# Low parts of the state-space input weights: computed beside the first MLP and loaded from DRAM

## The chip, the cores and the metric

One core of a Trainium2 chip runs the whole program in one launch. The metric is the device time of one execution in microseconds, from the median of several runs. TensorE (PE) does the matmuls, VectorE (DVE), ScalarE (ACT) and GpSimd (POOL) the elementwise work, and SyncE's queue (SP) issues every DMA of the kernel before the change. Each engine takes its instructions in the order in which they are written into its queue; a waiting instruction holds up all that stand behind it.

## The reference, cut to what matters

A trunk of two layers on 512 tokens of width 1024, in float32. Layer 0 is attention and an MLP, layer 1 a state-space mixer and an MLP:

```python
for i in range(DEPTH):                      # DEPTH = 2
    mix = attention_mixer(x, ...) if i % 2 == 0 else mamba2_bidir_mixer(x, ...)
    x = layer_norm(DN_ALPHA * x + mix, ln1_g[i], ln1_b[i])
    x = layer_norm(DN_ALPHA * x + squared_relu_mlp(x, mlp_w1[i], mlp_w2[i]), ln2_g[i], ln2_b[i])

def squared_relu_mlp(x, w1, w2):            # 1024 -> 4096 -> 1024
    return jnp.square(jax.nn.relu(x @ w1)) @ w2

def mamba2_bidir_mixer(x, w_in, ...):
    zxbcdt = x @ w_in                       # 1024 -> 6208: the state-space input weights
    z, xbc, dt = jnp.split(zxbcdt, ...)
    xbc = jax.nn.silu(depthwise_conv_centred(xbc, conv_w, conv_b))
    ...                                     # one chunked scan per direction, gate, grouped norm
    return y @ w_out
```

## The kernel before

Every float32 matmul is made of three float32r matmuls: both operands are split into a high part (a rounded copy) and a low part (what the rounding left), and `split3` (L208) adds high times high, high times low and low times high into one PSUM bank. The weights are streamed as 219 chunks of 128x1024 float32 (512 KB), in the order of their use: chunks 0 to 25 for attention, 26 to 89 for the first MLP, 90 for the time steps (half a chunk), 91 to 138 for the state-space input projection, 139 to 154 for its output projection, 155 to 218 for the second MLP. One chunk feeds 24 matmuls of 512 columns.

`Weights.prepare` (L54) brings one chunk in: SP loads `w_raw`, ACT copies it to `w_hi` (L69), and DVE subtracts to get `w_lo` (L70); for the chunks listed in `ON_POOL` (L27) POOL does that subtraction. Chunks sit in a pool of four buffers; `more_weights` (L261) opens a second pool beside it, of four buffers in the first MLP, so that eight chunks are on their way there. In the state-space stage only the four are left.

`Main` (L250) holds the token-major phases. `sweep` (L274) multiplies and adds into the residual, `norm` (L328) is the layer norm of one tile of 128 tokens (its `rstd` on POOL, L336; the scaling on DVE, L340 and L343), `transpose` turns a normed tile for the next phase, with its low part taken on DVE at L232, `first_tiles` begins the next phase while the last tokens are still being normed, and `mlp` (L375) runs four quarters of eight up chunks and eight down chunks.

`ssd` (L757) is the state-space stage, eight groups. In each group the 48 projection chunks of the stage are fed to PE between the group's own small matmuls, in an order fixed by a table of step numbers (L971). POOL makes the decay differences `e` and `tb` from rows `r` that DMAs broadcast from `ac_d` (L865 to L875), the masks `m` and `tu` (L984 to L987) and the chunk states `pv` (L1064); DVE makes the convolutions (L801), `cbl` and `cbu` (L1025, L1026), the weighted inputs `xw` (L1046), and the sum into `pv` (L1067). A grouped norm goes through DRAM: `rs_d` is written and read back (L938, L939), and DVE L947 waits for it.

PE's order is the order of the code. The other engines' orders, and SP's, are set by a scheduler at build time; a change in any of their work moves what stands around it.

Of the kernel before, what the change touches and what calls it, by code (L numbers as in the profile page):

```python
# [40 lines left out]
class Weights:  # L41
    """Weight chunks of [128, 1024] float32, streamed in order and split exactly into two float32r parts."""

    def __init__(self, nc, pool, sources, ahead, in_order):
        self.in_order = in_order
        self.nc = nc
        self.pools = [pool]
        self.ahead = ahead
        self.sources = sources
        self.ready = []  # L50
        self.wide_until = 0
        self.at = 0

    def prepare(self, after=(), between=None):  # L54
# [7 lines left out]
        n = src.shape[1]  # L62
        raw = pool.tile([P, 1024], F32, name="w_raw")
# [14 lines left out]

    def widen(self, pool, extra, n):
        """Has a second pool of so many buffers take its share of the next n chunks to be used."""  # L80
# [13 lines left out]
class Slots:  # L94
    """Room for the two parts of eight [128, 512] operand tiles."""
# [16 lines left out]
def tile_encoder_trunk(ctx: ExitStack, tc: tile.TileContext, a: dict, out: bass.AP, stop=None):  # L112
# [14 lines left out]
    def banks_of(stack, counts):  # L127
        """Further PSUM banks: counts maps a name to its number of banks."""
# [11 lines left out]
    def in_order(ins, first):  # L140
        """Has an engine issue ins behind first."""
# [92 lines left out]
    def sweep_lead(yh, yl, banks, chunks, n, first=0):  # L234
        """Chunks of y @ W into four banks, K tile by K tile."""
# [13 lines left out]
    # ------------------------------------------------------------------ token-major phases  # L249
    class Main:  # L250
# [23 lines left out]
        def sweep(self, yh, yl, scale_res, finish=None, begun=None, within=None, between=None):  # L274
            """res <- [ALPHA *] res + y @ W for the K tiles in yh/yl; finish(t) when a token tile is done,
            within() late in the last one."""
# [83 lines left out]
        def first_tiles(self, n, m=P, then=None):  # L360
            """The next phase's first n projections, by token halves while the last tokens get done."""
# [39 lines left out]
        def overlapped(self, then=None):  # L401
            """Has token tiles 0 and 1 turned while 2 and 3 are computed."""
# [9 lines left out]
    # ------------------------------------------------------------------ layer 0: attention  # L412
    def attention(stack):
        """Returns the eight operand tiles of the output projection and its first sweep, begun."""
# [50 lines left out]
        # value rows of the neighbourhood heads, gathered into the column blocks' windows  # L465
# [17 lines left out]
        # keys and values of the windowed heads  # L483
# [240 lines left out]
    # ------------------------------------------------------------------ layer 1: SSD mixer  # L724
# [3 lines left out]
    def step_sizes(main, ps):  # L728
        """dt_tok <- softplus(dt + bias), tokens on partitions; wdec <- dt * -exp(A_log)."""
# [563 lines left out]
```

## Time and profile before

| | |
|---|---|
| runs, us | 1487.74, 1493.44, 1494.26 (median 1493.44) |
| span of the profiled execution, us | 1492.0 |
| PE busy | 1408.6 us, 94% of the span |
| DVE, ACT, POOL busy | 883.1, 583.6, 448.6 us |
| moved by DMA | 161.37 MB, 108 GB/s over the span |

The span runs from the first to the last instruction of one profiled execution; its own time outside the profiler is not given, so the span stands for it, 1.4 us under the median. Busy PE time counts pipelined matmuls and can't fall much; what can be lost or won lies in the 6% in which PE waits, and in the stage where it does. Waits are put down to the instruction that came last. Of the stages, attention ends at about 230 us, the first MLP at about 590, the state-space stage's groups run from about 640 to 1040, and the second MLP ends the program.

### The profile page before, as it was taken

The numbers are of one execution on the slowest core, as the hardware profiler recorded it, in microseconds if no ns is written. First come the engines' busy times: TensorE is split into PE (matmuls) and PEld (weight loads), VectorE is DVE, ScalarE is ACT, GpSimd is POOL, SyncE is SP. The second block draws the span as 40 slices with busy tenths as digits, with TensorE's granted clock in tenths as the row PEclk, the third lists the DMA queues.
The fourth block names the chain that finished last, engine by engine and source line by source line (L and its number), as shares of the span: only waits on it lengthen the run. The fifth ranks groups of instructions, "written<-read, shape, count | busy, mean of one in ns | idle before, by whom it ended". The sixth has DMA issues, their size and how long they took to land.

```text
span 1492.0 us, 18850 instructions
## 1 busy us (share of the span) xinstructions
PE 1408.6 (94%) x7200; PEld 1160.6 (78%) x7200; DVE 883.1 (59%) x1267; ACT 583.6 (39%) x899; POOL 448.6 (30%) x347
## 2 busy tenths in 40 slices
PE   8899999999999999978888997898998999999997
PEld 7777778888888888866777776776888888888886
DVE  4577576444343437598788788977467444243336
ACT  5688633223132321444444545452324323142220
POOL 1354230000000121276576777665333100000000
PEclk9999999999999999999999999998999999999999
DMA  8322255323232212363434443321436333143101
GB/s 286 104 87 63 71 200 168 99 90 95 68 129 86 78 56 78 117 195 100 138 110 125 130 134 121 99 89 43 139 109 226 99 99 99 57 128 99 57 1 57
DMA packets 62259, 161.37 MB, mean 108 GB/s; under 512 B 9596, under 2 KB 19480, under 8 KB 62168
## 3 DMA queue, kind: packets, MB, share of 16 engines
q1 hardware_dynamic: 62168, 160.16, 34.2%
q8 instruction: 57, 0.93, 0.3%
q14 instruction: 34, 0.28, 0.1%
HBM read 154.73 MB, written 5.39 MB: 107 GB/s over the span
## 4 chain that ended last, share of the span: by engine, by line
PE 70%; DVE 10%; POOL 7%; DMA 6%; issue 4%; SPq 2%; ACT 1%; DVEq 0%; POOLq 0%; ACTq 0%
PE mm L209 17%; PE mm L210 17%; PE mm L211 16%; PE b L211 4%; PE b L210 4%; PE b L209 4%; DMA r<-ac_d 4%; POOL m L987 1%; DVE w_lo L70 1%; DVE xw L1046 1%; POOL tu L985 1%; DVE res L343 1%; DVE lo L232 1%; POOL m L984 1%; SPq L509 1%
## 5 line engine op out<-in xcount | busy, mean ns | idle before, releaser
L69 ACT ACTIVATE w_hi<-w_raw 128x1024 fp32r<-128x1024 f32 (+1 forms) x220 | 231.6, 1054 | 585.6 <-PE mm L210 279.7
L209 PE MATMUL mm<-hi,w_hi 128*128 128x512 f32 (+2 forms) x1112 | 431.1, 388 | 0.6 <-ACT hi L231 0.5
L210 PE MATMUL mm<-lo,w_hi 128*128 128x512 f32 (+2 forms) x1112 | 421.2, 379 | 10.2 <-DVE lo L232 10.2
L211 PE MATMUL mm<-hi,w_lo 128*128 128x512 f32 (+2 forms) x1112 | 418.8, 377 | 0.0
L70 DVE TENSOR_TENSOR w_lo<-w_raw,w_hi 128x1024 fp32r<-128x1024 f32 (+1 forms) x182 | 235.1, 1294 | 266.4 <-ACT w_hi L69 265.8
L210 PEld LDWEIGHTS mm<-lo,w_hi 128*128 128x128 f32 (+1 forms) x1112 | 213.4, 192 | 44.2 <-DVE lo L232 10.9
L209 PEld LDWEIGHTS mm<-hi,w_hi 128*128 128x128 f32 (+1 forms) x1112 | 213.1, 192 | 41.1 <-issue 5.3
L211 PEld LDWEIGHTS mm<-hi,w_lo 128*128 128x128 f32 (+1 forms) x1112 | 212.9, 191 | 39.6
L70 POOL TENSOR_TENSOR w_lo<-w_raw,w_hi 128x1024 fp32r<-128x1024 f32 (+1 forms) x38 | 94.2, 2481 | 448.9 <-ACT w_hi L69 442.9
L209 PE MATMUL mm<-w_hi,hi 128*128 128x512 f32 x352 | 142.2, 404 | 5.7 <-ACT hi L171 5.0
L211 PE MATMUL mm<-w_hi,lo 128*128 128x512 f32 x352 | 140.3, 398 | 1.6 <-DVE lo L232 1.6
L210 PE MATMUL mm<-w_lo,hi 128*128 128x512 f32 x352 | 140.2, 398 | 0.0
L210 PE MATMUL b<-w_lo,hi 128*128 128x512 f32 (+1 forms) x328 | 123.5, 377 | 0.6 <-DVE w_lo L70 0.6
L211 PE MATMUL b<-w_hi,lo 128*128 128x512 f32 (+1 forms) x328 | 123.5, 376 | 0.0
L209 PE MATMUL b<-w_hi,hi 128*128 128x512 f32 (+1 forms) x328 | 123.5, 376 | 0.0
L336 POOL TENSOR_TENSOR rstd<-ve,half 128x1 f32<-128x1 f32 x16 | 12.5, 784 | 328.3 <-DVE neg L334 310.2
L209 PEld LDWEIGHTS mm<-w_hi,hi 128*128 128x128 f32 x352 | 67.4, 191 | 20.9 <-ACT hi L171 5.0
L211 PEld LDWEIGHTS mm<-w_hi,lo 128*128 128x128 f32 x352 | 67.3, 191 | 18.1 <-DVE lo L232 2.5
L210 PEld LDWEIGHTS mm<-w_lo,hi 128*128 128x128 f32 x352 | 67.4, 192 | 14.3
L384 DVE TENSOR_TENSOR sq<-relu 128x512 f32<-128x512 f32 x64 | 60.3, 943 | 28.7 <-ACT relu L382 28.7
L210 PEld LDWEIGHTS b<-w_lo,hi 128*128 128x128 f32 x328 | 61.8, 188 | 13.0 <-DVE w_lo L70 1.0
L209 PEld LDWEIGHTS b<-w_hi,hi 128*128 128x128 f32 x328 | 61.7, 188 | 12.0
(284 smaller groups left out, 1952.0 us busy)
## 6 DMA issues: line engine op xcount, KB each, us to landing
w_raw<-in_w_m_dram SPq DMA_DIRECT2D x128, 512.0 KB, 3.6
w_raw<-in_w_ssm_dram SPq DMA_DIRECT2D x48, 512.0 KB, 3.6
r<-ac_d SPq DMA_DIRECT2D x64, 256.0 KB, 4.5
w_raw<-in_w_so_dram SPq DMA_DIRECT2D x16, 512.0 KB, 3.5
w_raw<-in_w_att_dram SPq DMA_DIRECT2D x14, 512.0 KB, 4.9
r<-ac_d SPq DMA_DIRECT2D x64, 96.0 KB, 2.9
w_raw<-in_w_ao_dram SPq DMA_DIRECT2D x8, 512.0 KB, 3.7
xraw<-in_xT_dram SPq DMA_DIRECT2D x8, 256.0 KB, 6.4
```

Of the source, the lines that this page charges most:

```text
L69: split = [nc.scalar.activation(hi[:, cols], raw[:, cols], AF.Copy), eng.tensor_tensor(lo[:, cols], raw[:, cols], hi[:, cols].bitcast(F32) ...
L70: eng.tensor_tensor(lo[:, cols], raw[:, cols], hi[:, cols].bitcast(F32), op=ALU.subtract)]
L209: PE.matmul(ps, lhs_h, rhs_h, start=first, stop=False)
L210: PE.matmul(ps, lhs_h, rhs_l, start=False, stop=False)
L211: PE.matmul(ps, lhs_l, rhs_h, start=False, stop=last)
L232: return DVE.tensor_tensor(lo, src, hi.bitcast(F32), op=ALU.subtract)
L343: self.last = DVE.scalar_tensor_tensor(self.res[t][:, cols], u, rstd, self.b[:, cols], op0=ALU.mult, op1=ALU.add),
L384: DVE.tensor_tensor(s, r, r, op=ALU.mult)
L509: nc.sync.dma_start(out=vj[r * 32:r * 32 + 32, j, kt, :], in_=vb_g[kt * 4 + r, NA_START[j]:NA_START[j] + 32, pair * P:pair * P + P])
L984: POOL.tensor_tensor(m, cbl, bc(dt_tok[:, :, hf:hf + 1], full), op=ALU.mult)
L985: POOL.tensor_tensor(t, cbu, bc(dt_tok[:, :, 32 + hf:33 + hf], full), op=ALU.mult)
L987: POOL.tensor_tensor(m, m, es[h], op=ALU.mult)
```

## The change

The low parts of the 48 chunks 91 to 138 are no longer subtracted when they are used. While the first MLP runs, each call of `prepare` also takes one step of a generator, `split_beside`: SP loads a state-space chunk (`pre_raw`), ACT makes its high part (`pre_top`), POOL subtracts (`pre_low`), and SP stores the result in DRAM (`w_low`). Two buffers of each serve these steps; to make room, the second weight pool of the first MLP shrinks from four buffers to two. In the state-space stage SP loads `w_raw` and ACT makes `w_hi` as before, and a DMA issued by POOL loads `w_lo` from DRAM. `ON_POOL` is unchanged; its entries for chunks 91 to 138 have no more use. The docstrings and comments that the diff removes are left out here.

```diff
     def __init__(self, nc, pool, sources, ahead, in_order):
...
+        self.split_at = {}
+        self.beside = None
...
         n = src.shape[1]
+        if self.beside is not None:
+            next(self.beside, None)
+        if self.at - 1 in self.split_at:
+            raw = pool.tile([P, 1024], F32, name="w_raw")
+            hi = pool.tile([P, 1024], F32R, name="w_hi")
+            lo = pool.tile([P, 1024], F32R, name="w_lo")
+            nc.gpsimd.dma_start(out=lo, in_=self.split_at[self.at - 1])
+            nc.sync.dma_start(out=raw, in_=src)
+            nc.scalar.activation(hi, raw, AF.Copy)
+            self.ready.append((hi, lo))
+            return
...
+    def split_beside(self, pool, dram, indices):
+
+        nc = self.nc
+        for i in indices:
+            src = self.sources[i]
+            raw = pool.tile([P, 1024], F32, name="pre_raw")
+            top = pool.tile([P, 1024], F32R, name="pre_top")
+            low = pool.tile([P, 1024], F32, name="pre_low")
+            nc.sync.dma_start(out=raw, in_=src)
+            nc.scalar.activation(top, raw, AF.Copy)
+            nc.gpsimd.tensor_tensor(low, raw, top.bitcast(F32), op=ALU.subtract)
+            kept = dram.tile([P, 1024], F32, name=f"w_low{i}")
+            nc.sync.dma_start(out=kept, in_=low)
+            self.split_at[i] = kept
+            yield
...
-            main.more_weights(4, 68)
+            main.more_weights(2, 68)
...
             main.sweep(yh, yl, True, begun=begun, **main.overlapped())
+            pre = tc.tile_pool(name="pre", bufs=2)
+            weights.beside = weights.split_beside(pre.__enter__(), dram, range(91, 139))
...
+            run(weights.beside)
+            weights.beside = None
+            pre.__exit__(None, None, None)
```

What the scheduler makes of it stands at three places; the numbers of lines differ between the two programs. PE's order is the same in both, row for row.

POOL between attention and the first MLP, before. The four `rstd` are those of the four token tiles after attention, and the `w_lo` are chunks 26 to 29:

```order
L336 TENSOR_TENSOR rstd<-ve,half 128x1
L70 TENSOR_TENSOR w_lo<-w_raw,w_hi 128x1024 x2
L336 TENSOR_TENSOR rstd<-ve,half 128x1 x2
L70 TENSOR_TENSOR w_lo<-w_raw,w_hi 128x1024 x2
L336 TENSOR_TENSOR rstd<-ve,half 128x1
```

The same place of the same queue, now:

```order
L365 TENSOR_TENSOR rstd<-ve,half 128x1
L83 TENSOR_TENSOR w_lo<-w_raw,w_hi 128x1024 x2
L102 TENSOR_TENSOR pre_low<-pre_raw,pre_top 128x1024
L365 TENSOR_TENSOR rstd<-ve,half 128x1
L102 TENSOR_TENSOR pre_low<-pre_raw,pre_top 128x1024
L365 TENSOR_TENSOR rstd<-ve,half 128x1
L102 TENSOR_TENSOR pre_low<-pre_raw,pre_top 128x1024
L83 TENSOR_TENSOR w_lo<-w_raw,w_hi 128x1024 x2
L365 TENSOR_TENSOR rstd<-ve,half 128x1
```

Three of the new subtractions have come to stand between the norms; one is ahead of the second tile's `rstd`, and after the third tile's `rstd` three subtractions follow where there were two.

SP in the first MLP, before, is one run of loads:

```order
L271 DMA ln_g<-in_ln_dram 128x1024
L272 DMA ln_b<-in_ln_dram 128x1024
L68 DMA w_raw<-in_w_m_dram 128x1024 x52
L68 DMA w_raw<-in_w_dt_dram 128x512
```

Now stores and loads of the new steps stand between them (twelve rows out of its middle):

```order
L104 DMA w_low_3513<-pre_low 128x1024
L100 DMA pre_raw<-in_w_ssm_dram 128x1024
L81 DMA w_raw<-in_w_m_dram 128x1024
L104 DMA w_low_3558<-pre_low 128x1024
L100 DMA pre_raw<-in_w_ssm_dram 128x1024
L104 DMA w_low_3603<-pre_low 128x1024
L100 DMA pre_raw<-in_w_ssm_dram 128x1024
L104 DMA w_low_3648<-pre_low 128x1024
L100 DMA pre_raw<-in_w_ssm_dram 128x1024
L104 DMA w_low_3693<-pre_low 128x1024
L100 DMA pre_raw<-in_w_ssm_dram 128x1024
L104 DMA w_low_3738<-pre_low 128x1024
```

Each store waits for POOL's subtraction, and the next load of the pair stands behind it; from the first `pre_raw` to the last store there are 48 steps and 44 loads of MLP chunks, and the last 15 MLP chunks are loaded behind the last store.

POOL in one group of the state-space stage, now; the DMA rows are new, and the subtractions of `w_lo` that stood in this queue and in DVE's are gone:

```order
L1016 TENSOR_TENSOR m<-m,e 128x512
L901 TENSOR_TENSOR e<-r,ac_tok 128x512
L71 DMA w_lo<-w_low_4283 128x1024
L1093 TENSOR_TENSOR pv_7801<-pv_7771,cdec 128x512
L901 TENSOR_TENSOR e<-r,ac_tok 128x512
L903 TENSOR_TENSOR tb<-r,ac_tok 128x512 x2
L71 DMA w_lo<-w_low_4328 128x1024
L959 TENSOR_TENSOR rstd<-rstd,half 128x4
```

Such a DMA waits until PE has done with the chunk that held its buffer, four chunks earlier, and the group's own work on POOL stands behind it.

## Rows read from the trace of the kernel before

**Rows 1.** The page: busy time by engine, and the chain that ended last.

```profile
PE 1408.6 (94%) x7200; PEld 1160.6 (78%) x7200; DVE 883.1 (59%) x1267; ACT 583.6 (39%) x899; POOL 448.6 (30%) x347
PE 70%; DVE 10%; POOL 7%; DMA 6%; issue 4%; SPq 2%; ACT 1%; DVEq 0%; POOLq 0%; ACTq 0%
```

**Rows 2.** Windows: stretch, length, busy PE, PEld, DVE, ACT, POOL; clock, DMA share, GB/s.

```profile
180.00:235.00 55.00, 47.79 (x292) 39.99 (x292) 42.13 (x75) 18.14 (x31) 17.33 (x11) 0.94 0.51 172
235.00:545.00 310.00, 310.00 (x1427) 256.30 (x1426) 131.76 (x143) 97.33 (x124) 14.41 (x6) 1.00 0.29 93
545.00:640.00 95.00, 90.68 (x553) 79.38 (x551) 55.60 (x97) 25.32 (x34) 21.91 (x16) 1.00 0.34 105
640.00:985.00 345.00, 302.90 (x1653) 246.20 (x1654) 283.03 (x332) 168.84 (x232) 244.81 (x184) 0.96 0.42 124
```

**Rows 3.** PE's waits from 640 to 985 us: total us, times, longest.

```profile
PE aux L1056 <- DVE xw L1046: 16.0, 12, 2.3
PE aux L899 <- DVE cbu L1026: 11.6, 5, 3.9
PE aux L899 <- ACT xs L811: 6.1, 1, 6.1
PE aux L916 <- DVE pv L1067: 4.9, 3, 4.1
```

**Rows 4.** Groups of DVE and POOL, 640 to 985 us: count, busy us, mean ns, idle before.

```profile
L70 DVE TENSOR_TENSOR w_lo<-w_raw,w_hi 128x1024 fp32r<-128x1024 f32 x34 | 49.9, 1467 | 1.5 <-ACT w_hi L69 1.5
...
L987 POOL TENSOR_TENSOR m<-m,e 128x512 f32<-128x512 f32 x27 | 45.0, 1671 | 11.0 <-DVE m L986 11.0
L874 POOL TENSOR_TENSOR tb<-r,ac_tok 128x512 f32<-128x512 f32 x30 | 37.8, 1261 | 52.4 <-DMA r<-ac_d 46.8 <-DVE w_lo L70 3.1 <-DVE r L999 2.4
...
L70 POOL TENSOR_TENSOR w_lo<-w_raw,w_hi 128x1024 fp32r<-128x1024 f32 x5 | 12.9, 2573 | 2.6 <-ACT w_hi L69 2.6
...
L930 POOL TENSOR_TENSOR rstd<-rstd,half 128x4 f32<-128x4 f32 x6 | 6.1, 1021 | 2.4 <-DVE rstd L929 2.4
```

**Rows 5.** The chain that ended last, by line, 640 to 985 us.

```profile
by line: DMA r<-ac_d 13.9%; issue 10.9%; POOL m L987 5.8%; PE mm L209 5.3%; POOL tu L985 5.2%; PE mm L210 5.0%; PE mm L211 4.7%; POOL m L984 4.4%; DVE xw L1046 4.0%; POOL tb L874 3.8%; POOL pv L1064 3.3%; DVE w_lo L70 3.1%; POOL e L872 2.9%
```

**Rows 6.** DVE and PE around one group's start: start us, us, then idle before.

```profile
844.78 2.18 DVE L947 SCALAR_TENSOR_TENSOR hi<-hi,nw,q 128x512 f32<-128x512 f32 x2 [1.04 <-DMA q<-rs_d]
...
850.12 1.88 DVE L70 TENSOR_TENSOR w_lo<-w_raw,w_hi 128x1024 fp32r<-128x1024 f32 x1
...
857.49 2.09 DVE L1046 TENSOR_TENSOR xw<-xtok,wdec 128x384 f32<-128x384 f32 x2
859.63 1.38 PE L1056 MATMUL aux<-xw,btok 128*128 128x128 f32 x10 [0.83 <-DVE xw L1046]
```

**Rows 7.** Attention's last norms: DVE, then POOL, then PE.

```profile
214.67 1.41 DVE L343 SCALAR_TENSOR_TENSOR res<-ln_u,rstd,ln_b 128x512 f32<-128x512 f32 x2
...
220.49 5.28 DVE L343 SCALAR_TENSOR_TENSOR res<-ln_u,rstd,ln_b 128x512 f32<-128x512 f32 x2
219.95 5.26 POOL L70 TENSOR_TENSOR w_lo<-w_raw,w_hi 128x1024 fp32r<-128x1024 f32 x2
227.53 0.58 PE L210 MATMUL mm<-lo,w_hi 128*128 128x256 f32 x1 [5.29 <-DVE lo L232]
```

**Rows 8.** First MLP: two drains one chunk apart; ACT's copies; DMA landings; one SP issue.

```profile
304.35 0.69 DVE L310 SCALAR_TENSOR_TENSOR res<-res,b 128x512 f32<-128x512 f32 x1 [3.23 <-PE b L211]
309.89 0.69 DVE L310 SCALAR_TENSOR_TENSOR res<-res,b 128x512 f32<-128x512 f32 x1 [4.85 <-PE b L211]
L69 ACT ACTIVATE w_hi<-w_raw 128x1024 fp32r<-128x1024 f32 x56 | 59.4, 1061 | 207.2 <-PE mm L210 97.5 <-PE b L211 53.8 <-PE mm L211 50.9
w_raw<-in_w_m_dram SPq DMA_DIRECT2D x128, 512.0 KB, 3.6
res<-in_x_dram SPq DMA_DIRECT2D x4, 512.0 KB, 6.1
229.75 0.33 SPq L271 DMA_DIRECT2D ln_g<-in_ln_dram  x1
```

## The prediction on record

> **What bounds the kernel now.** I began with the page: PE is busy for 94% of the span and holds 70% of the chain that ended last [rows 1]. What PE does isn't touched, so the question is where it waits. The windows by stage answer that [rows 2]. In the first MLP PE never stops: 310 of 310 us, with the DMA engines at a 0.29 share, ACT busy for a third and POOL for a twentieth of the time. There is room for other work, but also nothing to win. In the state-space stage, 640 to 985 us, PE is busy for 302.9 of 345 us, so some 42 us are lost; DVE is busy for 283.0 and POOL for 244.8. The list of PE's waits names DVE for nearly all of them: 16.0 us for `xw`, 11.6 for `cbu`, 4.9 for `pv`, and 6.1 once, at the start, for `xs` [rows 3]. On DVE the subtractions that the change removes are the largest group, 34 of 1.467 us; five more are on POOL [rows 4].
>
> That DVE is named doesn't mean that its load is the cause, so I looked at the chain of that stretch [rows 5]. `w_lo` on DVE is only 3.1% of it. The largest part is the broadcast `r<-ac_d`, 13.9%, and the six POOL lines shown add up to 25.4%. One group's start shows both sides [rows 6]: DVE runs a `w_lo` of 1.88 us right before the `xw` for which PE then waits, and there the removal helps; but shortly before, DVE stood still for the DMA `q<-rs_d` ahead of L947, and what comes behind that, `cbu` among it, would have been no earlier without any `w_lo`.
>
> **The state-space stage, term by term.** Of the 48 subtractions, 39 lie in the stretch (34 and 5); the nine earlier ones lie where PE is busy for 90.7 of 95 us [rows 2], and I take nothing for them.
> - Off DVE: 3.1% of 345 us is 10.7 us of chain. Taken: -10.7.
> - Off POOL: 12.9 us of work [rows 4]. How much of POOL's work lies on the chain: L987 has 5.8% of 345, or 20.0, of its 45.0 us there, L874 13.1 of 37.8, so 0.44 and 0.35 [rows 4, 5]; I use 0.4. Taken: -5.2.
> - DVE and POOL hold each other up. After attention two scalings that take 1.41 us on DVE took 5.28 while POOL did two subtractions in 5.26 [rows 7]. In the stage POOL's other 179 instructions average (244.8 - 12.9) / 179 = 1.296 us, where its smallest takes 1.02 [rows 2, 4]: 49 us of excess. `w_lo` is 49.9 of DVE's 283.0 us, 18%, and more of what reads two tiles at once; I take a quarter: 49 x 0.25 x 0.4 = -4.9, with 0 as the other end.
> - Added to POOL: 39 DMA issues. The trace has none on this engine. Below stands SP's issue of 0.33 us [rows 8], above the subtraction that it replaces, 2.57 us [rows 4]; nearest is the POOL instruction that moves almost nothing, 1.02 us [rows 4]. 39 x 1.02 x 0.4 = +15.9, with ends of +5.1 and +40.1. Behind each on POOL stand `pv`, `tb` and the masks, and DVE and then PE wait for those.
> - Added to the DMA engines: 39 x 0.524 MB = 20.4 MB, or 59 GB/s on top of 124 GB/s, which were a 0.42 share [rows 2]: about 0.20 more. `r<-ac_d` is 48 us of the chain. If each finds that much more of the engines taken, it costs 9.6 us; if the loads fall beside it, nothing. Taken: +4.
>
> The sum is -0.9 us, with ends at -15.7 and +34. The landing of `w_lo` itself I cost at nothing: 3.6 us for 512 KB [rows 8], against the three chunks of 5.54 us that PE works between the release of a buffer and its next use (5.54 us lie between two drains of the first MLP [rows 8]); it costs what exceeds that if POOL comes to the issue over 12 us late. SP's queue loses nothing here, since the new loads are POOL's.
>
> Two rules of the Trainium skill bear on these terms. On the price of an issue: POOL's own reads are held up by DVE, as rows 7 show for the other direction. The page "SBUF — State Buffer", section "Who interferes with whom", has DVE instructions with two SBUF inputs contend with a GpSimd instruction that reads SBUF, not with one that only writes it; writing descriptors is no read, so by this rule the issue costs its 1.02 us, and by POOL's average of 1.296 it would add another 4.3 us. On the DMA term: by the page "DMA: Bandwidth & Descriptors", section "Issuing engines are not separate DMA queues", what POOL issues runs on the same 16 engines and interleaves; were POOL's queue apart, the term would be 0 and the sum -4.9. No row here shows a POOL DMA beside an SP one.
>
> **Between attention and the first MLP.** PE waits 5.29 us there for a low part that DVE could only make after those held-up scalings [rows 7]. In the new order three subtractions follow that tile's `rstd` where there were two, so the scalings are held up by up to 2.57 us more; another new one stands ahead of the second tile's `rstd`, and delays a norm with some slack, for which I take 1. Taken: +3.5, from 0 (DVE gets in between) to +8 (all three add up).
>
> **In the first MLP.** The 48 steps move 1.57 MB with each MLP chunk where 0.524 MB went. A full share is 93 / 0.29 = 321 GB/s [rows 2], so one transfer occupies the engines for 1.63 us, three for 4.9 of the 5.54 us that a chunk takes PE. ACT and POOL have the time: 1.06 and 2.57 us a step. But with two buffers a step waits for the last but one: two SP issues 0.66, the store ahead of it 1.63, landing 3.6, ACT 1.06, POOL 2.57, together 9.5 us for two steps, 4.76 a step. The order has 48 steps beside 44 MLP chunks: 44 x 5.54 / 48 = 5.08 us a step. It fits by 0.3 us. What covers a late step: the MLP's chunks are split ahead, by two chunks at the end of a sweep, some 11 us. A step that falls behind is felt because `pre_top` stands in ACT's queue ahead of `w_hi` and the MLP's own activations, and DVE and PE wait for those; the stores stand ahead of MLP loads on SP. Taken: +2, from 0 (nothing shows) to +33 (below).
>
> **The sum.** -0.9 + 3.5 + 2 = +4.6 us on the span of 1492.0, or 1496.6; the median of the runs shown is 1.4 us above that span, so 1498.
>
> **The rivals.**
> - Faster: the issue on POOL is as cheap as SP's, loads fall beside the broadcasts, and the MLP hides its steps. Then -15.7 in the stage, and 0 to +3.5 for the norms: 1478 to 1481. For it speaks that DVE is the busiest engine beside PE and stands right ahead of `xw`, PE's longest wait; against it, that POOL and its broadcasts hold more of the chain than DVE's `w_lo`.
> - Slower, in the first MLP: the steps set the pace. If `pre_raw` lands after 6.1 us, as the residual's loads did under load [rows 8], a step takes 6.0 us, the steps fall behind by 48 x 0.93 = 45 us, less 11 us of cover: +33. Halfway, at 5.2 us, it is 48 x 0.48 - 11 = +12. It decides from about 4.7 us: there 0.23 us a step use up the 11 us. Middle: +22, 1518. For it speaks a DMA share near 0.9; against it, that the stretches with several steps in a row have no MLP load between them.
> - Slower, in the state-space stage: an issue holds POOL, with its wait for PE's release, as long as the subtraction did on it, 2.57 us. That is +24 on the sum: 1522. For it speaks that all 39 now stand on POOL, where there were five; against it, that these waits were nearly nothing for the subtractions (1.5 us for 34 on DVE [rows 4]).
> That the subtractions would stay where they are is no rival: the order shows none of them left in the stage.
>
> **How the numbers follow.** The forecast, 1498, has 0.38, with a range of its own of 1490 to 1503; the faster case 0.27; the MLP's pace 0.20; POOL's hold 0.15. No change means within 0.5%, about what a measurement of this kernel can tell: 1486.0 to 1500.9. The faster case is faster; of the forecast's chance 0.36 lie within, 0.02 above; with the two slower cases that is 0.37 slower. The range leaves out a tenth at either end: 1477, the best case less a little, to 1523, the middle of the two slower ones.
>
> **What would show it.** In the profile after: PE's wait for `xw` well under 16 us, that for `cbu` not; POOL's DMA issues with a duration of their own near 1 us; more of the chain in `r<-ac_d` and POOL; PE's wait before 230 us longer than 5.3 us; the first MLP's PE still without waits and a DMA share of 0.8 to 0.9. I am wrong if PE waits for ACT or for weights in the first MLP, if a POOL issue costs over 2 us, or if PE's waits in the state-space stage fall by more than 16 us.

## The result, and the profile after the change

The changed kernel takes 1510.75 us (median of four executions, 1510.41 to 1511.23) where the kernel before took 1492.74: a ratio of 1.0134, with a 95% interval of 1.0113 to 1.0155. That is 18.0 us slower. The forecast of 1498 was too low by 13; the range, 1477 to 1523, holds the time, and the likeliest case was not the one that came. The profiled execution of after has a span of 1509.4 us.

To see where the 18 us arise, I lined the two traces up by PE's work, which is the same in both: the start of the same matmul or transpose in after, less its start in before. It comes out at +0.7 us at the first transposes after attention (213.7 us in before), +6.8 when the first MLP is under way (239.9), +19.9 in its last sweep (564.1; its matmuls end at about 588), +18.4 where the state-space stage begins (623.3), +17.4 at that stage's end (1035.2) and +17.5 at the end of the program. So the transition costs about 6 us and the first MLP 13, some 1.5 come back ahead of the state-space stage, that stage costs nothing in sum (-1.0), and the rest nothing.

The same windows as in [rows 2] for after; the last one is moved by 18 us, so that it covers the same work. Columns: stretch, length, busy PE, PEld, DVE, ACT, POOL; granted clock, DMA share, GB/s.

```profile
180.00:235.00 55.00, 42.53 (x256) 34.21 (x255) 41.50 (x68) 21.57 (x36) 24.96 (x15) 0.92 0.59 204
235.00:545.00 310.00, 300.17 (x1378) 249.13 (x1377) 177.11 (x139) 129.00 (x155) 120.09 (x48) 0.98 0.71 246
545.00:640.00 95.00, 94.77 (x548) 83.04 (x548) 50.67 (x86) 29.85 (x40) 15.79 (x16) 1.00 0.37 126
658.00:1003.00 345.00, 302.03 (x1656) 245.35 (x1657) 244.43 (x298) 169.15 (x232) 219.13 (x219) 0.96 0.62 185
```

In the MLP, where PE was busy for 310 of 310 us, 10 are now idle, and the DMA share has gone from 0.29 to 0.71. In the state-space stage DVE was relieved of 38.6 us (283.0 to 244.4) and POOL of 25.7, its new issues counted, and PE has gained nothing from it: busy for 302.03 us, where it was 302.90 in as long a stretch.

**The first MLP.** PE's waits from 235 to 545 us, then ACT's (total us, times, longest):

```profile
PE mm L238 <- ACT relu L411: 8.6, 3, 3.8
```

```profile
ACT pre_top L101 <- DMA pre_raw<-in_w_ssm_dram: 119.8, 42, 5.9
```

ACT is at work for only 129 of the 310 us, but it waits for 119.8 us, in 42 of the steps, for their `pre_raw` to land, and whatever stands behind `pre_top` waits with it. One place from ACT's timeline (start us, us, instruction, and in brackets the idle time before it and what ended it), and PE's two waits there:

```profile
378.42 1.06 ACT L101 ACTIVATE pre_top<-pre_raw 128x1024 fp32r<-128x1024 f32 x1 [2.62 <-DMA pre_raw<-in_w_ssm_dram]
379.38 1.04 ACT L82 ACTIVATE w_hi<-w_raw 128x1024 fp32r<-128x1024 f32 x1
380.32 0.58 ACT L411 ACTIVATE relu<-mm 128x512 f32<-128x512 f32 x1
...
383.24 1.06 ACT L101 ACTIVATE pre_top<-pre_raw 128x1024 fp32r<-128x1024 f32 x1 [1.67 <-DMA pre_raw<-in_w_ssm_dram]
384.20 1.04 ACT L82 ACTIVATE w_hi<-w_raw 128x1024 fp32r<-128x1024 f32 x1
385.14 0.58 ACT L411 ACTIVATE relu<-mm 128x512 f32<-128x512 f32 x1
```

```profile
380.96 0.50 PE L238 MATMUL mm<-w_hi,hi 128*128 128x512 f32 x1 [2.29 <-ACT relu L411]
385.78 0.79 PE L238 MATMUL mm<-w_hi,hi 128*128 128x512 f32 x1 [3.84 <-ACT relu L411]
```

A `relu` of 0.58 us, which only empties a bank for PE, comes as late as the DMA two instructions ahead of it. Three such waits are 8.6 us. The MLP loses 13, and most of the rest is the clock: behind two of these waits PE was granted less.

```profile
285.00:290.00 5.00, 2.49 (x11) 1.72 (x10) 4.08 (x4) 3.31 (x5) 2.60 (x2) 1.00 0.53 146
290.00:295.00 5.00, 5.00 (x16) 3.96 (x15) 2.80 (x3) 1.32 (x3) 0.86 (x2) 0.66 0.95 324
...
380.00:385.00 5.00, 0.98 (x3) 0.48 (x3) 3.84 (x3) 3.30 (x5) 2.54 (x2) 0.81 0.78 279
385.00:390.00 5.00, 4.22 (x10) 3.36 (x11) 4.58 (x3) 2.30 (x4) 3.64 (x2) 0.50 0.91 318
390.00:395.00 5.00, 5.00 (x23) 4.11 (x23) 1.18 (x1) 0.53 (x1) 0.63 (x1) 1.00 0.92 350
```

In these stretches the clock (last column but two) is at its upper level, 2.4 GHz, before the first wait; in the stretch behind it PE is busy all the time and gets 16 matmuls done instead of 23, at 0.66; from 385 to 390 us it runs at 0.50, the lower level, 1.2 GHz, and has it back by 390. (23 - 16) x 5 / 23 = 1.5 us are lost in the one, and half of the 4.22 busy us, 2.1, in the other; with all of PE's waits, 9.8 us, that is 13.4. The aligned traces have the loss in the same places: the lag grows by 1.7 us from 240 to 245 us (times of before), by 4.4 from 260 to 284 and by 8.7 from 360 to 370, and nowhere else; no weight comes late to PE.

**The state-space stage.** PE's waits from 658 to 1003 us, to be held against [rows 3]:

```profile
PE aux L1085 <- DVE xw L1075: 14.4, 11, 2.1
PE aux L928 <- DVE cbu L1055: 13.2, 5, 3.5
PE y L1025 <- DVE pv L1096: 6.7, 3, 5.0
```

`xw` still takes 14.4 us, where it took 16.0, though nothing of the weights stands on DVE any more. The groups (count, busy us, mean ns, idle before) and one group's start on DVE and POOL say why:

```profile
L1126 DVE TENSOR_TENSOR hi<-hi,z 128x512 f32<-128x512 f32 x8 | 26.0, 3252 | 2.7 <-POOL hi L1041 2.7
L1126 DVE TENSOR_TENSOR lo<-lo,z 128x512 f32<-128x512 f32 x4 | 14.9, 3728 | 0.0
...
L71 POOL DMA_DIRECT2D w_lo<-w_low x39 | 23.1, 593 | 0.0
```

```profile
867.38 0.68 DVE L1055 TENSOR_TENSOR cbu<-aux,trib 128x512 f32<-128x512 f32 x1
867.98 6.76 DVE L1126 TENSOR_TENSOR hi<-hi,z 128x512 f32<-128x512 f32 x1
...
867.52 0.57 POOL L71 DMA_DIRECT2D w_lo<-w_low  x1
868.11 1.06 POOL L903 TENSOR_TENSOR tb<-r,ac_tok 128x512 f32<-128x512 f32 x1
869.12 3.05 POOL L1013 TENSOR_TENSOR m<-cbl,dt_tok 128x512 f32<-128x512 f32 x3
872.14 2.05 POOL L1014 TENSOR_TENSOR tu<-cbu,dt_tok 128x512 f32<-128x512 f32 x2
874.14 0.60 POOL L71 DMA_DIRECT2D w_lo<-w_low  x1
```

L1126 multiplies a group's y with its gate z. Its eight on `hi` took 10.5 us before the change (1.318 each) and take 26.0 now, and this one 6.76, from POOL's `tb` until 0.55 us after the last of POOL's six tensor instructions. Five of its calls, one in each of five groups from 763 to 971 us, take 6.76 to 6.78. POOL is not slowed meanwhile: its three `m` take 3.05 us. From the same place in the kernel before, POOL and DVE:

```profile
849.87 4.50 POOL L984 TENSOR_TENSOR m<-cbl,dt_tok 128x512 f32<-128x512 f32 x3
...
849.52 0.68 DVE L1026 TENSOR_TENSOR cbu<-aux,trib 128x512 f32<-128x512 f32 x1
```

There the three took 4.50 us, and what stood behind `cbu` on DVE was a `w_lo` of 1.88 us [rows 6]. Now the multiply stands there, and behind it the convolutions and `xw`; before, the scheduler had it ahead of `cbl` (848.32 us). So POOL got its relief, and DVE gave its own back at another instruction.

### The profile page after: what moved, and what is told of

Its sections match the earlier page's. It is cut to its first block, busy times and chain, and to the rows that moved or that the text cites. A ratio compares the mean times of both kernels' runs of the same rounds, so it can differ in the third digit from the quotient of the medians.

```text
span 1509.4 us, 19200 instructions
## 1 busy us (share of the span) xinstructions
PE 1411.7 (94%) x7200; PEld 1162.5 (77%) x7200; DVE 894.8 (59%) x1227; ACT 628.3 (42%) x947; POOL 538.0 (36%) x435
## 4 chain that ended last, share of the span: by engine, by line
PE 62%; DVE 13%; DMA 11%; POOL 7%; issue 4%; SPq 2%; ACT 2%; DVEq 0%; POOLq 0%; ACTq 0%
PE mm L238 14%; PE mm L239 14%; PE mm L240 14%; PE b L240 4%; PE b L239 4%; PE b L238 4%; DMA r<-ac_d 4%; DMA pre_raw<-in_w_ssm_dram 3%; DMA q<-rs_d 2%; DVE hi L1126 1%; POOL m L1016 1%; DVE res L372 1%; DVE w_lo L83 1%; DVE lo L261 1%; POOL e L901 1%
## 5 line engine op out<-in xcount | busy, mean ns | idle before, releaser
L83 DVE TENSOR_TENSOR w_lo<-w_raw,w_hi 128x1024 fp32r<-128x1024 f32 (+1 forms) x142 | 209.6, 1480 | 244.3 <-ACT w_hi L82 243.9
L82 ACT ACTIVATE w_hi<-w_raw 128x1024 fp32r<-128x1024 f32 (+1 forms) x172 | 179.6, 1048 | 356.9 <-PE mm L239 138.5
L102 POOL TENSOR_TENSOR pre_low<-pre_raw,pre_top 128x1024 f32<-128x1024 f32 x48 | 120.6, 2514 | 121.5 <-ACT pre_top L101 121.5
L238 PE MATMUL mm<-w_hi,hi 128*128 128x512 f32 x352 | 144.2, 410 | 14.4 <-ACT relu L411 8.6
L83 POOL TENSOR_TENSOR w_lo<-w_raw,w_hi 128x1024 fp32r<-128x1024 f32 (+1 forms) x30 | 74.4, 2483 | 212.8 <-ACT w_hi L82 206.1
L101 ACT ACTIVATE pre_top<-pre_raw 128x1024 fp32r<-128x1024 f32 x48 | 50.9, 1060 | 128.1 <-DMA pre_raw<-in_w_ssm_dram 128.1
L413 DVE TENSOR_TENSOR sq<-relu 128x512 f32<-128x512 f32 x64 | 67.5, 1055 | 22.4 <-ACT relu L411 22.4
L239 PEld LDWEIGHTS mm<-w_lo,hi 128*128 128x128 f32 x352 | 68.4, 194 | 14.4
```

Of the source, the lines that this page charges most:

```text
L82: split = [nc.scalar.activation(hi[:, cols], raw[:, cols], AF.Copy), eng.tensor_tensor(lo[:, cols], raw[:, cols], hi[:, cols].bitcast(F32) ...
L83: eng.tensor_tensor(lo[:, cols], raw[:, cols], hi[:, cols].bitcast(F32), op=ALU.subtract)]
L101: nc.scalar.activation(top, raw, AF.Copy)
L102: nc.gpsimd.tensor_tensor(low, raw, top.bitcast(F32), op=ALU.subtract)
L238: PE.matmul(ps, lhs_h, rhs_h, start=first, stop=False)
L239: PE.matmul(ps, lhs_h, rhs_l, start=False, stop=False)
```

## The experiments

The kernels run on several chips; each comparison is with the kernel before on the same chip (medians of 1491.6 to 1492.1 us there). Behind the texts on record, each paragraph has the median, the ratio with its interval, and what the aligned trace shows. Times of the alignment are those of the kernel before.

**1. Two buffers alone.**

```
-            main.more_weights(4, 68)
+            main.more_weights(2, 68)
```

> The kernel before, with the second weight pool of the first MLP and the transition cut from four buffers to two, as the change does to make room. Theory A (the 48 steps themselves pace the first MLP through ACT's queue) expects no loss: 1492.7 plus or minus 2, PE without waits between 260 and 545 us. Rival B (the MLP's 13 us come from the smaller pool, since a chunk is then split ahead less far) expects those 13 us here: about 1505, with PE waiting for w_lo or w_hi in the MLP.

Measured: 1489.48 us, ratio 0.9982 (0.9967 to 0.9998). PE has no wait between 260 and 545 us; the lag on the kernel before is 0.4 us at 564.1, and the program ends 0.7 us earlier. Rival B falls: the smaller pool costs the MLP nothing. At 239.9 the lag is 2.0 us here, and 1.5 in the kernel of 7, which has neither steps nor the smaller pool; so 2 us in the transition of a single profiled execution say little.

**2. A later start in the program's text.**

```
                     for i, ps in enumerate(self.first_tiles(first)):
                         act(ps, i)
+                    begun()
...
-            weights.beside = weights.split_beside(pre.__enter__(), dram, range(91, 139))
+            beside = weights.split_beside(pre.__enter__(), dram, range(91, 139))
...
+                lambda: setattr(weights, "beside", beside))
```

> The changed kernel, but the 48 steps begin only behind the first projections of the MLP, so that none stands between attention and the MLP. If the 6.8 us lost there come from POOL's subtractions between the norms, they go: PE's wait for the norm before 240 us back from 6.9 to about 5.3 us, the transposes of t at the times of before (within 1 us), total 1510.75 - 6.8 = 1504 if the MLP loses its 13 us as it does now. More steps are then left to the MLP's end, where nothing of the MLP loads beside them; if they hold up the first chunks of the next stage, up to 12 x 2.57 = 31 us come back there, and the end of the MLP shows it. Rival (the 6.8 us come from the smaller pool or from the DMA traffic of the norms' residuals): still 6 to 7 us late at 240 us, total unchanged at 1511.

Measured: 1513.31 us, ratio 1.0155 (1.0111 to 1.0199), no better than the change. The edit didn't do what it was meant to: the first `pre_low` ran at 211.52 us, where it ran at 213.53, so the steps began no later, although their calls stand later in the text. It tells nothing of the transition; the last but one kernel (11) does.

**3. The loads alone.**

```
+            weights.split_at = {i: sources[i] for i in range(91, 139)}
-            weights.beside = weights.split_beside(pre.__enter__(), dram, range(91, 139))
```

> The 48 steps are taken out, the four buffers are back, and in the state-space stage the second operand is loaded by POOL from the weights themselves: the low parts are not computed (the product then counts the weights twice), but its loads, their size and their queue are those of the changed kernel. So this is the change's effect on the state-space stage alone. Theory A (there the relief of DVE and POOL is given back by DMA contention and by DVE's gate multiply standing behind POOL's train, as the alignment of the two traces says: -0.9) expects 1492 plus or minus 3. Rival D (the stage gains, and the gain is hidden by something that the late arrival of the MLP causes) expects 1476 to 1482. The multiply of y with z on DVE should take about 3 us in the mean here too.

Measured: 1494.19 us, ratio 1.0017 (1.0001 to 1.0033). The state-space stage by itself gains nothing from the change; rival D falls. The multiply is held here too:

```profile
L1126 DVE TENSOR_TENSOR hi<-hi,z 128x512 f32<-128x512 f32 x8 | 24.7, 3083 | 2.0 <-POOL hi L1041 2.0
```

**4. The steps alone.**

```
-            self.split_at[i] = kept
```

> The 48 steps run as in the changed kernel, stores included, but the state-space stage splits its weights as before and loads no low part. So this is the cost of the transition and of the first MLP alone. Theory A expects 1492.7 + 6.8 + 13.0 - 1.1 = 1511 (1508 to 1514), the transposes of t 6.8 us late and the MLP's end 19 us late as in the changed kernel. If the loads in the state-space stage themselves cost what their relief gains by chance, nothing else changes; were the stage to gain from them (rival D), this would be 1520 or more.

Measured: 1516.2 us, ratio 1.0173 (1.0146 to 1.0199): +24 us, 2 more than expected at the upper end. The transition and the MLP lose what they lose in the changed kernel (+7.6 us at 239.9, +21.3 at 564.1), and the stage then neither gains nor loses much (+20.5 to +22.2). By this kernel the loads are worth 5 us to the stage, by the one before they cost 2; the two don't add up to the changed kernel's 18 us, and the difference, some 8 us, is left unexplained. That the slowdown arises ahead of the state-space stage doesn't hang on it.

**5. Three buffers for the raw chunks.**

```
-            raw = pool.tile([P, 1024], F32, name="pre_raw")
-            top = pool.tile([P, 1024], F32R, name="pre_top")
+            raw = pool.tile([P, 1024], F32, name="pre_raw", bufs=3)
+            top = pool.tile([P, 1024], F32R, name="pre_top", bufs=1)
```

> The changed kernel with three buffers for pre_raw and one for pre_top, where it has two of each. Theory A (pre_top stands in ACT's queue and waits there for the landing of a load that was issued only when the last but one buffer came free, 5.6 us before) expects ACT's wait for pre_raw to fall from 120 us to under 40 in the first MLP, PE's waits for relu to vanish, and 8 to 13 us back: 1498 to 1503. Rival C (the three transfers a step saturate the DMA engines, whose share is 0.71) expects nothing back: 1511, with ACT waiting as long, since a load issued earlier then lands later.

Measured: 1504.52 us, ratio 1.0081 (1.0066 to 1.0097): 6 us back, less than expected. ACT's waits in the MLP:

```profile
ACT pre_top L101 <- POOL pre_low L102: 86.4, 34, 10.2
...
ACT pre_top L101 <- DMA pre_raw<-in_w_ssm_dram: 3.3, 1, 3.3
```

The wait for the landing is gone, 119.8 us to 3.3, with as many bytes moved (245 GB/s against 246), so rival C's limit by bandwidth falls. But `pre_top` now has one buffer, and ACT waits for POOL to read it, 86.4 us: the place in ACT's queue still holds `relu`, for another reason. PE still waits 6.5 us for it.

**6. The gate multiply ahead of `cbl`.**

```
-                DVE.tensor_tensor(ys[j], ys[j], tiles.pop(("z", g, j)), op=ALU.mult)
+                gated = DVE.tensor_tensor(ys[j], ys[j], tiles.pop(("z", g, j)), op=ALU.mult)
...
-            DVE.tensor_tensor(cbl, cps_v, bc(trif.unsqueeze(1), full), op=ALU.mult)
+            cbl_ins = DVE.tensor_tensor(cbl, cps_v, bc(trif.unsqueeze(1), full), op=ALU.mult)
+            if g > 0:
+                in_order(cbl_ins, gated)
```

> The changed kernel with one order set by hand on DVE: a group's cbl is issued behind the last multiply of y with z of the group before, which in the changed kernel runs behind cbl and cbu and is held 6.8 us while POOL works through a train of seven instructions. If that multiply is what takes the relief of DVE back, its mean falls from 3.3 to under 2 us, PE's wait for xw from 14.4 to under 8 us, and the stage gains 4 to 10 us: 1501 to 1507. Rival (the multiply is held in either place, or cbl and so cbu come later by as much; the r broadcasts set the pace): 1508 to 1516.

Measured: 1495.06 us, ratio 1.0013 (0.9996 to 1.0029): 15.7 us less than the changed kernel, more than expected. PE's waits for `xw` from 640 to 1010 us, and the multiply:

```profile
PE aux L1087 <- DVE xw L1077: 0.8, 1, 0.8
...
L1128 DVE TENSOR_TENSOR hi<-hi,z 128x512 f32<-128x512 f32 x8 | 6.9, 867 | 5.0 <-POOL hi L1041 5.0
```

The multiply is at 0.87 us, `xw` comes in time, and the lag on the kernel before shrinks group by group from 21.2 us (623.3) to 3.3 (1035.2): the stage now gains 18. So one instruction's place on DVE had eaten the stage's gain.

**7. No second operand at all.**

```
-            nc.gpsimd.dma_start(out=lo, in_=self.split_at[self.at - 1])
-            self.ready.append((hi, lo))
+            self.ready.append((hi, hi))
```

> The kernel before without any low part for the 48 weight chunks of the state-space stage: no steps beside the MLP, no subtraction, no load; the product takes the high part twice (the correction by the low parts is left out). So it is the relief of DVE and POOL alone, without its price in DMA traffic and POOL issues; beside the run that only loads (1494) the difference is that price. By the sum on record the relief is 10.7 + 5.2 + 4.9 = 20.8 us and its price 19.9: 1472. If the stage does not gain from the relief (PE waits for broadcasts and for work on POOL that is there either way) it stays near 1490.

Measured: 1469.63 us, ratio 0.9842 (0.9826 to 0.9858): the relief alone is 22.5 us, and the loads take 24.6 of it back (1494.19 - 1469.63). The multiply takes 0.95 us here, but not because POOL is idle. It stands elsewhere in DVE's queue, between two convolutions, and where it runs beside POOL's train it is POOL that is held up:

```profile
792.01 0.83 DVE L1124 TENSOR_TENSOR hi<-hi,z 128x512 f32<-128x512 f32 x1
792.25 1.50 POOL L1011 TENSOR_TENSOR m<-cbl,dt_tok 128x512 f32<-128x512 f32 x1
```

So the 24.6 us hold the other order on DVE as well as the loads. The broadcasts land sooner than with the loads (size, median us from issue to landing, 640 to 1010 us; this kernel, then the changed one):

```profile
r<-ac_d SPq DMA_DIRECT2D x57, 256.0 KB, 4.3
r<-ac_d SPq DMA_DIRECT2D x55, 96.0 KB, 2.8
```

```profile
w_lo<-w_low POOLq DMA_DIRECT2D x40, 512.0 KB, 4.8
r<-ac_d SPq DMA_DIRECT2D x64, 256.0 KB, 5.6
r<-ac_d SPq DMA_DIRECT2D x63, 96.0 KB, 5.1
```

**8. `pre_top` made by POOL.**

```
-            nc.scalar.activation(top, raw, AF.Copy)
+            nc.gpsimd.tensor_copy(top, raw)
```

> The changed kernel with pre_top made by POOL in place of ACT: the same loads, stores and buffers, and nothing of the steps in ACT's queue. Theory A expects ACT to wait for no pre_raw, PE's waits for relu to vanish and the first MLP to lose under 4 us instead of 13: about 1501, unless POOL, with some 5 us a step instead of 2.6, falls so far behind that SP holds the MLP's own loads behind pre_raw's, which would show as PE or DVE waiting for w_raw. Rival C (DMA traffic) expects the 13 us unchanged: 1511.

Measured: 1496.25 us, ratio 1.0028 (1.0014 to 1.0043): 14.5 us back, with the same loads, stores and buffers. From 235 to 545 us:

```profile
235.00:545.00 310.00, 307.37 (x1427) 256.41 (x1427) 212.10 (x151) 93.58 (x119) 194.61 (x95) 0.99 0.72 250
```

PE waits for no `relu`, and does in this stretch the 1427 matmuls that it did before [rows 2], with the DMA share as high as ever, 0.72. The lag stays where the transition left it: +8.9 us at 239.9, +8.2 at 564.1. POOL now waits for the landings in ACT's place, 101.3 us, and PE's only wait in the stretch is 2.6 us, for DVE. So it is ACT's queue, not the traffic. Of the transition's loss nothing is gone.

**9. The gate order in the kernel before.**

The edit of 6, made in the kernel before:

```
+            if g > 0:
+                in_order(cbl_ins, gated)
```

> The kernel before with the same order by hand on DVE that gave the changed kernel 15.7 us (cbl behind the last gate multiply of the group before). If that order only mends what the change brought (the multiply took 1.3 and 1.1 us in the mean before, 3.2 and 3.1 after), there is nothing to gain here: 1490 to 1496. Rival (the order is better in itself, and the change has no share in it): 1478 to 1486.

Measured: 1489.0 us, ratio 0.9979 (0.9968 to 0.9989), just below what was expected. The order is worth 3 us by itself and 15.7 with the change: it mends mainly what the change brought.

**10. Both repairs.**

> The changed kernel with both repairs, which act in different stages: pre_top made by POOL, and the gate multiply ahead of cbl on DVE. If the two causes are separate, their gains add up: 1510.75 - 14.5 - 15.7 = 1480.5 (1477 to 1485), 12 us faster than the kernel before. If the second gain was only the first one's delay given back in the waits of the state-space stage, they don't: about 1495.

The edits of 6 and 8 together. Measured: 1480.34 us, ratio 0.9914 (0.9887 to 0.9942). The sum held, so the two causes are separate. What is left ahead of the stage is the transition: +8.9 us at 239.9, +7.9 at 564.1.

**11. Both repairs, and POOL's first step behind the last `rstd`.**

The edits of 6 and 8, and:

```
-            POOL.tensor_tensor(rstd, ve, half, op=ALU.pow)
+            self.root = POOL.tensor_tensor(rstd, ve, half, op=ALU.pow)
...
-            nc.gpsimd.tensor_copy(top, raw)
+            self.in_order(nc.gpsimd.tensor_copy(top, raw), behind)
...
-            weights.beside = weights.split_beside(pre.__enter__(), dram, range(91, 139))
+            weights.beside = weights.split_beside(pre.__enter__(), dram, range(91, 139), main.root)
```

> The kernel with both repairs, and POOL's first step held behind the last rstd between attention and the MLP, so that nothing of the steps runs on POOL among the norms. If the 6 to 8 us lost between attention and the MLP come from the steps on POOL standing ahead of rstd and beside DVE's scalings, 5 to 7 us come back: 1473 to 1476, the transposes of t within 2 us of the times of before. If they come from the steps' transfers beside the residual's, nothing does: 1480. The steps then end about 25 us later, at 560 us, still ahead of the last norms of the MLP.

Measured: 1473.5 us, ratio 0.9878 (0.9853 to 0.9903), the fastest of those that compute the whole: 18 us under the kernel before and 37 under the changed one. At 239.9 the lag is -0.2 us. POOL among the norms, in the changed kernel and then in this one:

```profile
213.53 2.38 POOL L102 TENSOR_TENSOR pre_low<-pre_raw,pre_top 128x1024 f32<-128x1024 f32 x1
215.88 1.00 POOL L365 TENSOR_TENSOR rstd<-ve,half 128x1 f32<-128x1 f32 x1
216.85 2.54 POOL L102 TENSOR_TENSOR pre_low<-pre_raw,pre_top 128x1024 f32<-128x1024 f32 x1
223.01 0.55 POOL L365 TENSOR_TENSOR rstd<-ve,half 128x1 f32<-128x1 f32 x1 [3.61 <-DVE neg L363]
223.53 2.60 POOL L102 TENSOR_TENSOR pre_low<-pre_raw,pre_top 128x1024 f32<-128x1024 f32 x1
226.08 5.55 POOL L83 TENSOR_TENSOR w_lo<-w_raw,w_hi 128x1024 fp32r<-128x1024 f32 x2
233.99 0.55 POOL L365 TENSOR_TENSOR rstd<-ve,half 128x1 f32<-128x1 f32 x1 [2.36 <-DVE neg L363]
```

```profile
212.09 0.56 POOL L365 TENSOR_TENSOR rstd<-ve,half 128x1 f32<-128x1 f32 x1 [2.38 <-DVE neg L363]
217.64 1.11 POOL L365 TENSOR_TENSOR rstd<-ve,half 128x1 f32<-128x1 f32 x1 [4.99 <-DVE neg L363]
218.73 5.26 POOL L83 TENSOR_TENSOR w_lo<-w_raw,w_hi 128x1024 fp32r<-128x1024 f32 x2
227.12 1.11 POOL L365 TENSOR_TENSOR rstd<-ve,half 128x1 f32<-128x1 f32 x1 [3.14 <-DVE neg L363]
```

From the second `rstd` to the fourth it is 18.1 us in the changed kernel and 15.0 here, as before the change (213.32 to 228.36), and in the changed kernel the second was itself held behind a subtraction (215.88, right at the end of 213.53 + 2.38). Beside the subtractions DVE's pairs of scalings L369 take 3.1 to 3.5 us in the changed kernel, and 1.4 here.

The experiment bounds POOL's share and doesn't settle it. Of the 9.1 us between the lags of 10 and 11 at 239.9, 2.1 were there at 200 us, and 3.1 arose by 205, where in 10 DVE waits 2.3 us for a residual to land and in 11 0.4; all this lies ahead of POOL's first step. The other 3.8 us lie among the norms; there, two loads and two stores of the steps, which SP issues at 219 and 225 us in 10, move out together with POOL's work, but no engine but ACT waits for a transfer there. So some 4 us are shown for POOL's steps, in the repaired kernel, where a step puts two instructions on POOL. For the changed kernel, with its single subtraction, the cause is read from its trace and not separately run.

**12. The issues alone, without their traffic.**

```
-            nc.gpsimd.dma_start(out=lo, in_=self.split_at[self.at - 1])
-            self.ready.append((hi, lo))
+            nc.gpsimd.dma_start(out=lo[:, :8], in_=src[:, :8])
+            self.ready.append((hi, hi))
```

> The kernel without low parts in the state-space stage (the product takes the high part twice), but with POOL's DMA issue for each of the 48 chunks put back, loading 8 of 1024 columns that nobody reads: 128 rows as before, 32 bytes in each instead of 4 KB. So it is the issue on POOL without its traffic, on the same order of DVE as the run without it (1469.6). By the prediction's term, 0.4 of POOL's time in the stage is on the path: 39 issues of 0.59 us, measured, cost 9 us, so 1479, and the traffic with the held multiply the other 15 of the 24.6 us. If POOL has room for its issues: 1470 to 1472, and all of the price is the traffic and the multiply. The r broadcasts should land in 2.8 and 4.3 us as without loads.

Measured: 1474.19 us, ratio 0.9891 (0.9863 to 0.9919), with a profiled span of 1470.1 against 1469.9 without them. It is no test: since nobody reads these buffers, nothing held the issues back, and the trace has all 48 ahead of the stage (ns: shortest, median, longest; first and last start):

```profile
L71 POOL DMA_DIRECT2D w_lo<-in_w_ssm_dram x48: 527/535/755, 552.6 to 620.3; - x48
```

What an issue costs in the middle of POOL's work was not measured by itself. The alignment bounds it. From 623.3 to 1035.2 us the stage gains 22.5 us with no loads (7), and 18, 19 and 17.5 with loads and issues in the three kernels with the repaired order (6, 10, 11): issues and traffic together then cost some 4 to 5 us, or up to 8 if the 3 us that the order is worth by itself are put to its account. With the order repaired, POOL's issues do wait, 9.0 and 9.3 us in 6 and 11, most of it for PE to release a buffer (7.9 and 7.7 us); those waits are part of this cost.

The lag on the kernel before, in us, at the same PE instructions (one profiled execution each; starts in the kernel before at the head):

```
                    213.7  239.9  564.1  623.3  760.5  909.8 1035.2 1461.8
changed kernel        0.7    6.8   19.9   18.4   16.9   22.7   17.4   17.5
3 loads alone         0.0    0.0    0.0   -0.6    2.0    7.7    3.3    3.3
4 steps alone         1.4    7.6   21.3   20.5   18.6   22.5   22.2   22.1
5 three raw          -0.9    4.8   13.1   11.6   12.1   17.4   11.2   11.3
6 gate first         -0.9    5.9   22.6   21.2   17.5   11.3    3.3    3.0
7 no second           0.0    1.5    1.5    0.9   -8.1  -12.0  -21.6  -21.8
8 top on POOL         0.9    8.9    8.2    6.8    5.2    9.4    2.7    1.9
10 both               2.3    8.9    7.9    6.5    4.6   -1.6  -12.3  -12.5
11 both, late        -2.9   -0.2   -1.8   -3.2   -4.7  -11.0  -20.7  -21.6
```

## Why the prediction was right and wrong

**The step that failed is the +2 for the first MLP.** It measured +13. The mechanism was there, as a rival: a step waits for its landing, `pre_top` stands in ACT's queue ahead of `relu`, PE waits. The term was mis-sized by the landing. I took 3.6 us from [rows 8], a landing in an MLP whose DMA engines were at a 0.29 share; with three transfers a chunk the share is 0.71 and `pre_raw` lands after 5.7 us (median, 235 to 545 us). The working put the deciding point at 4.7 us, and a better reading was at hand: the row with 6.1 us, the only landing under load, stood in the same group and was given to the rival alone. At 5.7 us the rival's own formula would have said some +24; 13 came. The steps followed each other faster than it has them (47 gaps from 213.5 to 470.1 us, 5.46 us each, not 5.8), by which it would say +7, and they were done by 472.5, over 100 us ahead of the MLP's end in after. Nor did the loss come the way that the formula adds it up, as weights that fall behind until a cover of 11 us is used up: PE waited for no weight, but three times for a `relu` that stood behind a late landing. That +13 lies between the two sums is therefore no success of the formula. It also has no term for the clock behind a wait, 1.5 and 2.1 us at two places.

**Transition: +3.5 taken, 0 to +8 given, about +6 measured** (0.7 to 6.8). The cause is the one that the text names, subtractions on POOL among the norms, as far as the changed kernel's trace and, in part, run 11 show it: three subtractions follow the third `rstd`, one holds up the second, and `rstd` standing behind a subtraction was worth more than the 1 us that I took.

**State-space stage: -0.9 taken, -1.0 measured, by other terms.** That the sum came out is luck. The three gains, 20.8 together, agree in sum with the relief alone, 22.5 us (7); none was measured by itself. The price, 19.9, came out at 24.6 (3 less 7), but it isn't made as I made it. An issue on POOL takes 0.593 us, not 1.02, and in the changed kernel's stage POOL did not wait ahead of it (idle 0.0 in its row). Issues and traffic cost 4 to 8 us, not 19.9. The larger part, for which I had no term, is the gate multiply: moving it gave 15.7 us (6), 3 of which the order is worth without the change (9); what is left of the 24.6 beside issues and traffic would be 16 to 20. What misled me was to count the subtractions taken off DVE and not ask which instruction, with two SBUF inputs like them, moves up into their place beside POOL's train.

Here the Trainium skill, page "SBUF — State Buffer", section "Who interferes with whom", says that a DVE instruction with two SBUF inputs contends with a GpSimd instruction that reads SBUF. The trace agrees, and shows how uneven it can be: 6.76 us for the multiply against 1.02 for each of POOL's. An issue was not drawn out beside DVE's work: the 39 of the stage took 0.57 to 0.64 us each. The Trainium skill, page "DMA: Bandwidth & Descriptors", section "Issuing engines are not separate DMA queues", has the loads of both engines interleave on the same 16; here too the trace agrees: with POOL's loads beside them, SP's broadcasts of 96 KB land after 5.1 us instead of 2.8.

**The rivals.** "Faster" failed on the multiply, and would have been right on its own point: with loads that cost little and an issue nearer to SP's price than to 1.02 us, the kernel takes 1473.5 once the steps are out of the way and DVE's order is mended (11). "POOL's hold" fell: an issue is a quarter of 2.57 us and waits for nothing in the changed kernel's stage. Of the signs that the text named, the rise of PE's wait ahead of the MLP came (6.9 us, from 5.29), a share of 0.8 to 0.9 did not (0.71), PE's wait for `xw` stayed at 14.4 us, and the stated disproof, PE waiting for ACT in the first MLP, did come.

**Open.** Why the multiply is held through six POOL instructions, when `w_lo` in the same place took 1.88 us [rows 6] and slowed POOL instead, no run tells. The rows differ in who began: the multiply at 867.98, 0.13 us ahead of POOL's train (868.11), that `w_lo` at 850.12, 0.25 us behind the first `m` (849.87). The Trainium skill, page "SBUF — State Buffer", section "Who interferes with whom", has the order of issue decide who blocks, not the shape. The traces agree that it isn't the shape: the same multiply beside the same `m` took 6.76 us in the changed kernel and 0.83 in 7. On the order they settle nothing: in both kernels the multiply began ahead of the POOL instruction that ran beside it, by 0.13 and by 0.24 us (in 7 with another `m` already running), and it was held in the one while POOL was held in the other; no run here set the order of issue by itself. Nor is the share of issues and traffic within their 4 to 8 us known, nor the 8 us by which the loads and the steps alone add up to more than the change.

## What to carry to other kernels

Work put "beside" a stage that an engine keeps full is paid for in the queues of the helpers: an instruction that waits for a DMA must not stand ahead of one that frees a bank for PE, however idle its engine looks. Price such a wait with a landing under the load that the change itself makes. And when work is taken off an engine, look at what moves up into its place: one multiply of 0.7 us in a group, beside another engine's train, took back most of what the stage had won, and an order of one line gave 15.7 us.

## What the runs showed of the hardware

- A DVE instruction with two SBUF inputs took 6.76 us instead of 0.68 while POOL ran six tensor instructions back to back, at 1.02 us each, and ended 0.55 us after the last of them, in five groups alike. It isn't always so: in the kernel before, at that place, a DVE instruction took 1.88 us and POOL's `m` 1.5 each, and in 7 the same multiply took 0.83 us and the `m` beside it 1.50.
- A DMA issue on POOL of 128 rows of 4 KB holds POOL for 0.593 us, with rows of 32 bytes for 0.535.
- TensorE's granted clock fell from 1.00 to the lower level, 0.50, at 291 us, 1.5 us behind a wait of 2.5 us, and again from 383 us, within a wait of 3.8 us that followed one of 2.3; by matmuls done, the wait of 2.5 us cost 4.
